# Up projection: all eleven middle gated tiles by seven block products, three of four weight sums on GpSimd, rows with the norm used a tile later

## The chip, the cores and the metric

One NeuronCore of a Trainium2 chip runs the whole kernel. The metric is the device time of one execution in microseconds. The engines are TensorE (PE in the profile; its weight loads are PEld), VectorE (DVE), ScalarE (ACT), GpSimd (POOL) and SyncE (SP), which issues the transfers.

## What is computed

One layer of a streaming encoder for 544 tokens (512 of a prompt, 32 of a decoded chunk), width 1024. Attention comes first; the change lies in the feed-forward part behind it:

```python
x = x + mixed @ w_out
f, conv_state = conv_ffn(rmsnorm(x, n2), w_up, conv_w, conv_b, w_down, conv_prev)

def conv_ffn(h, w_up, conv_w, conv_b, w_down, prev):
    u = h @ w_up                                  # 1024 -> 2 * 2816
    up = jnp.concatenate([prev.astype(u.dtype), u], axis=1)
    c = conv_b + conv_w[0] * up[:, 0:t]
    for j in range(1, CONV_W):                    # CONV_W = 3
        c = c + conv_w[j] * up[:, j:j + t]
    a, g = jnp.split(c, 2, axis=-1)
    return (jax.nn.gelu(a, approximate=False) * g) @ w_down, up[:, -(CONV_W - 1):]
```

The last two rows of `up` of the prompt and of the chunk are outputs too.

## The kernel before

Features lie on the 128 partitions and the 544 tokens along the free axis, in two halves of 272 (`HALVES`). Each float32 operand is split in a high part, rounded for TensorE's fast float32 format, and a low part, the rest; a product is three matmuls, high by high, high by low and low by high (`triple`). The high part is made by a cast on ScalarE or GpSimd, the low part by a subtraction on VectorE (`split`, lines 438 and 439; for weight tiles `prep`, lines 207 to 210).

**The up projection** makes 44 tiles of 128 features: 22 gated tiles, each of a value tile and a gate tile (`gate_order`, the loop of line 1118, index `n`). An ordinary tile (`conv`) takes one weight tile of 512 KB, 2 halves x 8 slices x 3 matmuls of 272 columns, and leaves PSUM by two copies into `us[0]` or `us[1]`. The first `RESCALE2` of them are multiplied by rows without the norm's factor, and VectorE applies it on the way out of PSUM (line 958); from then on the moving rows hold it (`plain`, made by `with_norm`) and ScalarE copies (line 960).

`conv_end` is the convolution for one tile: copies of the last rows into `state_u` on GpSimd, the first tap on ScalarE (line 944), the second on VectorE (line 945), two steps on GpSimd that mend the two columns at the seam between prompt and chunk (lines 947 and 948), the third tap on VectorE (line 950). Then a Gelu on ScalarE for the value tile, or the product with the value on VectorE for the gate tile (line 1128).

**A gated tile by seven block products** (`shared`, for `n` in `SHARED`) takes its value and gate tile together as a 2 x 2 block product over halves of the tokens and pairs of slices: 7 products of 4 slices x 3 matmuls in place of 8. It needs sums of weights (`sums_up`): of the four loaded blocks `wc`, `wd`, `wa`, `wb` (256 KB each) four sums s1 to s4 are made, and the seven operands are each split in high and low part. It needs sums of rows too (`form`), made once from `scaled_x`. ScalarE takes three of the products out of PSUM (lines 1057 to 1061), VectorE forms the four blocks of the result from PSUM and these (lines 1063 to 1070), and `conv_end` follows for both tiles.

**Order.** Engines work through their queues in order; a scheduler sets the order at build time by priorities. `ahead_up(6)` asks for weight operands so that six products' worth are made ahead of the product at hand, at a lower priority than the convolution. Transfers of this kind are issued one behind the other from SyncE. Buffers come from one pool of 50 (`fp`). From `n` = 17 on `take` also splits the gated tiles for the down projection.

Of the kernel before, what the change touches and what calls it, by code (L numbers as in the profile page):

```python
# [11 lines left out]
ALU = mybir.AluOpType  # L12
# [3 lines left out]
NP = 512  # L16
NS = 32
T = NP + NS
# [10 lines left out]
REST = GT - 2 * PAIRS  # L29
UNITS = PAIRS // 2  # L30
H = T // 2
SHARED = (7, 9, 11, 13, 15, 17)
AHEAD_UP = 6
TAKE = {17: 6, 18: 1, 19: 1, 20: 1, 21: 1}
HOMES = lambda g, f: [f] * 3 + [g] * 7 + [f] * 7 + [g] * 6 + [f] * 8 + [g] * 4 + [f] * 3 + [g] * 2
RESCALE2 = 6
EPS = 1e-6
NEG = -1e30
A_BLK = 80
# [109 lines left out]
def body(ctx, tc, a, o):  # L149
# [4 lines left out]
    V, G = nc.vector, nc.gpsimd  # L154
# [16 lines left out]
    def load(out, src, kind="x"):  # L171

        with tc.issue_after(loads[kind].ins) if kind in loads else nullcontext():
            loads[kind] = nc.sync.dma_start(out=out, in_=src)
# [16 lines left out]
    for n, i in enumerate(gate_order):  # L191
        if n not in SHARED:
            sources += [a["w_up"][i], a["w_up"][GT + i]]
# [109 lines left out]
    def col(name, i):  # L303
        return n1[:, i:i + 1] if name == "n1" else cols[:, COL[name][0] + i:COL[name][0] + i + 1]
# [81 lines left out]
    for step in START.split():  # L386
# [3 lines left out]
        else:  # L390
            c = {"": slice(0, T), "a": slice(0, HALVES[0][1]), "b": slice(HALVES[0][1], T)}[step[2:]]
# [45 lines left out]
    def split(dst_hi, dst_lo, src, e=V):  # L437
        nc.scalar.copy(dst_hi, src)  # L438
        e.tensor_tensor(dst_lo, src, rr(dst_hi), ALU.subtract)  # L439
# [485 lines left out]
    state_u = ft.tile([128, UT, 4], F32, name="state_u")  # L925
# [12 lines left out]
    late_g(carry[:, :, 0], carry[:, :, 0], t, ALU.add)  # L938

    def conv_end(m, u, done, own):  # L940
        G.tensor_scalar(state_u[:, m, 0:2], u[:, NP:NP + 2], 1.0, 1.0, ALU.mult, ALU.mult)  # L941
        G.tensor_scalar(state_u[:, m, 2:4], u[:, T:T + 2], 1.0, 1.0, ALU.mult, ALU.mult)
        c = own.tile([128, T], F32, name="s")
        act(c, u[:, 0:T], AF.Identity, scale=col("cw0", m), bias=col("cb", m))
        V.scalar_tensor_tensor(c, u[:, 1:T + 1], col("cw1", m), c, ALU.mult, ALU.add)

        G.tensor_scalar(c[:, NP:NP + 1], carry[:, m, 0:1], 1.0, 1.0, ALU.mult, ALU.mult)
        G.tensor_scalar(c[:, NP + 1:NP + 2], u[:, NP + 2:NP + 3], col("cw1", m), carry[:, m, 1:2],
                        ALU.mult, ALU.add)
        V.scalar_tensor_tensor(c, u[:, 2:T + 2], col("cw2", m), c, ALU.mult, ALU.add)  # L950
        done(c)

    def conv(m, n, done, own):
        u = us[n % 2]

        def evac(s, c0, cn, ps):
            if n < RESCALE2:
                V.tensor_tensor(u[:, 2 + c0:2 + c0 + cn], ps, rstd2[:, c0:c0 + cn], ALU.mult)
            else:
                nc.scalar.copy(u[:, 2 + c0:2 + c0 + cn], ps)  # L960
            if s == 1:
                conv_end(m, u, done, own)
        dense(evac, psa if n % 2 else psd)
# [5 lines left out]
    def with_norm(k):  # L969
        x = fp.tile([128, T], F32, name="s")  # L970
        V.scalar_tensor_tensor(x, x1[k], col("n2", k), rstd2, ALU.mult, ALU.mult)
        h, l = (fp.tile([128, T], F32R, name="s") for _ in range(2))
        split(h, l, x)
        scaled_x.append(x)
        plain.append((h, l))
# [8 lines left out]
    def form(j):  # L984
        t13, t24 = (fp.tile([128, T], F32, name="s") for _ in range(2))
        sums_of(scaled_x[2 * j], scaled_x[2 * j + 1], t13, t24)
        ops = {}
        for e, (names, t) in enumerate(((("t1", "t3"), t13), (("t2", "t4"), t24))):
            h, l = (xp.tile([128, T], F32R, name=f"x{p}{2 * j + e}") for p in "hl")
            split(h, l, t)  # L990
            for i, name in enumerate(names):
                ops[name] = tuple(x[:, i * H:i * H + H] for x in (h, l))
        for e, names in enumerate((("b11", "b12"), ("b21", "b22"))):
            for i, name in enumerate(names):
                ops[name] = tuple(x[:, i * H:i * H + H] for x in plain[2 * j + e])
        forms.append(ops)


    def sums_up():
        for n in range(len(SHARED)):  # L1000
            wc, wd, wa, wb = (fp.tile([128, T], F32, name="s")[:, :512] for _ in range(4))
            for e, w in enumerate((wc, wd, wa, wb)):
                load(w, a["w_shared"][n, :, 512 * e:512 * e + 512])
            s1, s2, s3, s4 = (fp.tile([128, T], F32, name="s")[:, :512] for _ in range(4))

            def both(x):
                h, l = (fp.tile([128, T], F32R, name="s")[:, :512] for _ in range(2))
                split(h, l, x)
                ready_up.append((h, l))
            both(wa)  # L1010
            yield
            V.tensor_tensor(s1, wc, wd, ALU.add)
            V.tensor_tensor(s2, s1, wa, ALU.add)
            both(s2)
            yield
            both(s1)
            yield
            V.tensor_tensor(s3, wc, wa, ALU.add)  # L1018
            both(s3)
            yield  # L1020
            both(wb)
            yield
            V.tensor_tensor(s4, s2, wb, ALU.add)
            both(s4)
            yield
            both(wd)
            yield

    ready_up, used_up = [], []
    making_up = sums_up()  # L1030

    def ahead_up(n):
        while len(ready_up) < len(used_up) + n:
            with tc.high_priority(LATER):
                if next(making_up, 0) == 0:
                    break

    def shared(m1, m2, nth, done1, done2, own):

        pool = psa if nth % 2 else psd  # L1040
        ba, bb, bc = (bank(pool)[:, :H] for _ in range(3))
        p0, q1, e = (ft.tile([128, 272], F32, name=x) for x in ("t_y", "t_b", "t_v"))
        (y11, y12), (y21, y22) = ((u[:, 2:2 + H], u[:, 2 + H:2 + T]) for u in us)
        tt = V.tensor_tensor

        def product(ps, name, first):
            ahead_up(AHEAD_UP)
            h, l = ready_up[len(used_up)]
            used_up.append(name)
            for j in range(KC // 2):  # L1050
                ks = slice(128 * j, 128 * j + 128)
                xh, xl = forms[j][name]
                mm(ps, lhsT=h[:, ks], rhs=xh, start=first and j == 0, stop=False, skip_group_check=True)
                mm(ps, lhsT=h[:, ks], rhs=xl, start=False, stop=False, skip_group_check=True)
                mm(ps, lhsT=l[:, ks], rhs=xh, start=False, stop=j == KC // 2 - 1, skip_group_check=True)
        product(bb, "b11", True)
        nc.scalar.copy(p0, bb)
        product(ba, "t2", True)
        nc.scalar.copy(q1, ba)
        product(bb, "t1", False)  # L1060
        nc.scalar.copy(e, bb)
        product(ba, "t3", False)
        tt(y22, ba, e, ALU.subtract)
        product(bc, "b21", True)
        tt(y11, bc, p0, ALU.add)
        product(bb, "b22", False)
        tt(y12, bb, q1, ALU.subtract)
        conv_end(m1, us[0], done1, own)
        product(ba, "t4", False)
        tt(y21, ba, p0, ALU.subtract)  # L1070
        conv_end(m2, us[1], done2, fp)


# [44 lines left out]
    for n, i in enumerate(gate_order):  # L1118
        part = []
        own = gp if n <= max(SHARED) else fp  # L1120

# [4 lines left out]
        def gate(c, part=part):  # L1126
            v = part[0]
            V.tensor_tensor(v, v, c, ALU.mult)
            gated.append(v)
        if n in SHARED:  # L1130
            shared(i, GT + i, SHARED.index(n), value, gate, own)
        else:
            for e, (m, done) in enumerate(((i, value), (GT + i, gate))):
                conv(m, tile_no, done, own if e == 0 else fp)
                if 1 <= tile_no <= 4:
                    with_norm(2 * tile_no - 2)
                    with_norm(2 * tile_no - 1)
                if tile_no == RESCALE2 - 1:
                    moving[:] = plain
                if RESCALE2 <= tile_no < RESCALE2 + 4:  # L1140
                    form(tile_no - RESCALE2)
                if tile_no >= RESCALE2 + 4 and len(used_up) < 7 * len(SHARED):
                    ahead_up(AHEAD_UP)
# [238 lines left out]
```

## Time and profile before

| what | value |
|---|---|
| median of 3 runs (lowest, highest) | 916.0 us (915.47, 920.13) |
| the profiled execution: time, span | 914.91 us, 913.1 us |
| TensorE busy | 888.1 us (97%) |
| VectorE busy | 743.7 us (81%) |
| ScalarE busy | 582.4 us (64%) |
| GpSimd busy | 421.0 us (46%) |
| granted TensorE clock, mean | 0.998 of full |

The span runs from the first to the last instruction. Busy time is the time in which an engine had at least one instruction under way; the start of one instruction may overlap the end of the one before it on the same engine. The up projection runs from about 536 to 797 us, and the stretch in which tiles by block products and ordinary ones alternate from 619.7 to 743 us.

### The profile page before, as it was taken

Reading aid. Unit: us, or ns where it says so; the run is one execution under the profiler, and the core shown is the slowest. Engines: PE = TensorE matmul, PEld = TensorE weight load, DVE = VectorE, ACT = ScalarE, POOL = GpSimd, SP = SyncE. Lnnn points to the kernel's source line nnn. Section 1 sums busy time; section 2 is a strip of 40 time slices with the busy share of each in tenths; the row PEclk is TensorE's granted clock in tenths of the full one; section 3 lists DMA queues with packets and bytes.
Section 4 is the critical chain, followed back from the end, with each engine's and each line's share of the span. In section 5 each row is a group of like instructions: output and inputs, shape, how many; then the busy total and the mean of one; then the engine's idle time right before and its main releaser. Section 6 shows DMA issues by size and latency. Waiting matters only on the chain.

```text
span 913.1 us, 18964 instructions
## 1 busy us (share of the span) xinstructions
PE 888.1 (97%) x7013; PEld 872.7 (96%) x7013; DVE 743.7 (81%) x1512; ACT 582.4 (64%) x1399; POOL 421.0 (46%) x577
## 2 busy tenths in 40 slices
PE   8979999999999999999999999999999999999998
PEld 7979899989989999999999999999999999999998
DVE  7798877768888897998865559998778778899996
ACT  5668787678878677777774236565555566645552
POOL 4625557465876777766551206444434344200100
PEclk9999999999999999999999999999999999999999
DMA  7222132322334443444415222253323012222342
GB/s 225 91 81 96 54 97 81 104 79 75 115 115 120 140 124 103 123 127 136 124 59 180 93 72 91 70 183 100 99 83 117 24 59 95 83 94 93 118 147 66
DMA packets 41742, 94.38 MB, mean 103 GB/s; under 512 B 5137, under 2 KB 16433, under 8 KB 41649
## 3 DMA queue, kind: packets, MB, share of 16 engines
q1 hardware_dynamic: 41648, 93.17, 32.5%
q8 instruction: 55, 0.90, 0.4%
q14 instruction: 39, 0.31, 0.1%
HBM read 80.48 MB, written 7.10 MB: 96 GB/s over the span
## 4 chain that ended last, share of the span: by engine, by line
PE 76%; DVE 9%; ACT 4%; POOL 4%; issue 2%; DVEq 0%; POOLq 0%; ACTq 0%
PE ps L90 73%; PE ps L94 3%; DVE q L454 1%; DVE zn L430 1%; ACT p L493 1%; DVE p L509 1%; POOL p L501 1%; DVE w_lo L210 1%; POOL t_sql L422 1%; POOL z L429 1%; DVE t_b L325 1%; DVE k L439 1%; POOL s L707 0%; POOL t_sqh L421 0%; DVE pt_l L520 0%
## 5 line engine op out<-in xcount | busy, mean ns | idle before, releaser
L90 PE MATMUL ps<-xh,w_lo 128*128 128x272 f32 x1024 | 297.5, 292 | 5.9 <-DVE w_lo L210 5.9
L90 PE MATMUL ps<-xh,w_hi 128*128 128x272 f32 x1024 | 297.5, 293 | 1.9 <-ACT z L420 1.7
L90 PE MATMUL ps<-xl,w_hi 128*128 128x272 f32 x1024 | 297.8, 292 | 0.3 <-DVE xl L333 0.3
L90 PE MATMUL ps<-s,w_hi 128*128 128x272 f32 x1088 | 205.3, 288 | 1.2 <-ACT w_hi L209 1.2
L90 PEld LDWEIGHTS ps<-xh,w_lo 128*128 128x128 f32 x1024 | 194.2, 190 | 7.2 <-DVE w_lo L210 6.7
L90 PEld LDWEIGHTS ps<-xh,w_hi 128*128 128x128 f32 x1024 | 193.9, 190 | 4.3 <-ACT z L420 2.0
L90 PEld LDWEIGHTS ps<-xl,w_hi 128*128 128x128 f32 x1024 | 194.5, 190 | 1.3 <-DVE xl L333 0.7
L90 PEld LDWEIGHTS ps<-s,w_hi 128*128 128x128 f32 x1088 | 169.9, 188 | 1.6 <-ACT w_hi L209 1.6
L90 PE MATMUL ps<-s,w_lo 128*128 128x272 f32 x544 | 154.1, 287 | 0.0
L210 DVE TENSOR_TENSOR w_lo<-w_raw,w_hi 128x1024 fp32r<-128x1024 f32 (+2 forms) x100 | 128.3, 1283 | 27.0 <-POOL w_hi L207 13.9
L90 PE MATMUL ps<-s 128*128 128x272 f32 (+1 forms) x843 | 115.2, 291 | 1.7 <-DVE s L379 1.7
L90 PEld LDWEIGHTS ps<-s 128*128 128x128 f32 x843 | 109.9, 189 | 2.2 <-DVE s L379 1.7
L207 POOL TENSOR_SCALAR w_hi<-w_raw 128x1024 fp32r<-128x1024 f32 (+2 forms) x62 | 67.0, 1081 | 92.6 <-PE ps L90 68.9
L90 PEld LDWEIGHTS ps<-s,w_lo 128*128 128x128 f32 x544 | 101.8, 188 | 0.1
L501 POOL TENSOR_SCALAR p<-p,rc 128x256 f32<-128x256 f32 (+3 forms) x128 | 74.9, 602 | 41.3 <-DVE rc L499 36.6
L941 POOL TENSOR_SCALAR state_u<-u 128x2 f32<-128x2 f32 x44 | 30.3, 689 | 118.0 <-ACT u L960 41.1
L493 ACT ACTIVATE p<-p,nm 128x256 f32<-128x256 f32 (+3 forms) x128 | 65.6, 516 | 27.9 <-DVE nm L490 27.8
L438 ACT CAST s<-s 128x512 fp32r<-128x512 f32 (+1 forms) x80 | 49.7, 633 | 39.1 <-DVE s L1018 10.6
L209 ACT CAST w_hi<-w_raw 128x1024 fp32r<-128x1024 f32 x38 | 40.0, 1053 | 44.6 <-PE ps L90 29.7
L439 DVE TENSOR_TENSOR s<-s 128x512 fp32r<-128x512 f32 (+1 forms) x80 | 55.7, 710 | 2.2 <-ACT s L438 2.1
L90 PE MATMUL ps<-k,q 128*128 128x256 f32 (+2 forms) x256 | 52.2, 308 | 2.6 <-DVE s L528 0.8
L422 POOL TENSOR_TENSOR t_sql<-t_sq,t_sqh 128x272 fp32r<-128x272 f32 x52 | 52.6, 1012 | 3.7
(175 smaller groups left out, 1801.1 us busy)
## 6 DMA issues: line engine op xcount, KB each, us to landing
w_raw<-in_w_in SPq DMA_DIRECT2D x50, 512.0 KB, 3.4
w_raw<-in_w_up SPq DMA_DIRECT2D x32, 512.0 KB, 3.4
w_raw<-in_w_pair SPq DMA_DIRECT2D x16, 512.0 KB, 3.4
s<-in_w_shared SPq DMA_DIRECT2D x24, 256.0 KB, 4.2
k<-k SPq DMA_DIRECT2D x40, 128.0 KB, 2.3
bias<-in_rel SPq DMA_DIRECT2D x16, 256.0 KB, 3.0
w_raw<-in_w_out SPq DMA_DIRECT2D x8, 512.0 KB, 3.5
s<-in_x SPq DMA_DIRECT2D x15, 272.0 KB, 5.8
```

The lines of the kernel that those rows point to most:

```text
L90: return self.nc.tensor.matmul(out, lhsT=lhsT, rhs=rhs, **kw)
L94: return self.nc.tensor.transpose(out, src, ident)
L207: G.tensor_scalar(hi[:, c], raw[:, c], 1.0, 1.0, ALU.mult, ALU.mult)
L209: nc.scalar.copy(hi[:, c], raw[:, c])
L210: V.tensor_tensor(lo[:, c], raw[:, c], rr(hi)[:, c], ALU.subtract)
L325: V.scalar_tensor_tensor(b, st, eps, b, ALU.add, ALU.mult)
L422: G.tensor_tensor(sql, sq, rr(sqh), ALU.subtract)
L438: nc.scalar.copy(dst_hi, src)
L439: e.tensor_tensor(dst_lo, src, rr(dst_hi), ALU.subtract)
L493: act(p[:, sl], p[:, sl], AF.Exp, bias=nm[:, t:t + 1], accum_out=sm[:, t:t + 1])
L501: G.tensor_scalar(p[:, sl], p[:, sl], rc[:, t:t + 1], 1.0, ALU.mult, ALU.mult)
L941: G.tensor_scalar(state_u[:, m, 0:2], u[:, NP:NP + 2], 1.0, 1.0, ALU.mult, ALU.mult)
```

## The change

`SHARED` names all of the gated tiles 7 to 17 in place of 7, 9, 11, 13, 15 and 17, so tiles 8, 10, 12, 14 and 16 are made by block products too, and no ordinary tile stands between them. The layout of the shared weights on the host follows `SHARED`. Of the four weight sums of a tile s1, s3 and s4 move from VectorE to GpSimd; s2 stays. `RESCALE2` goes from 6 to 7: a seventh ordinary tile is multiplied by rows without the norm's factor, and `form` and the first `ahead_up` come a tile later. The two copies into `state_u` become one instruction of two pieces of two columns.

```diff
-SHARED = (7, 9, 11, 13, 15, 17)
+SHARED = tuple(range(7, 18))
...
-RESCALE2 = 6
+RESCALE2 = 7
...
     def conv_end(m, u, done, own):
-        G.tensor_scalar(state_u[:, m, 0:2], u[:, NP:NP + 2], 1.0, 1.0, ALU.mult, ALU.mult)
-        G.tensor_scalar(state_u[:, m, 2:4], u[:, T:T + 2], 1.0, 1.0, ALU.mult, ALU.mult)
+        G.tensor_scalar(state_u[:, m].rearrange("p (e r) -> p e r", e=2),
+                        u[:, NP - 30:].rearrange("p (e c) -> p e c", e=2)[:, :, 30:], 1.0, 1.0, ALU.mult, ALU.mult)
...
-            V.tensor_tensor(s1, wc, wd, ALU.add)
+            G.tensor_tensor(s1, wc, wd, ALU.add)
             V.tensor_tensor(s2, s1, wa, ALU.add)
...
-            V.tensor_tensor(s3, wc, wa, ALU.add)
+            G.tensor_tensor(s3, wc, wa, ALU.add)
...
-            V.tensor_tensor(s4, s2, wb, ALU.add)
+            G.tensor_tensor(s4, s2, wb, ALU.add)
```

## Rows read from the trace of the kernel before

**Rows 1.** Windows: stretch, length, each engine busy us (instructions), PEclk, DMA.

```profile
619.70:743.00 123.30, 123.30 (x987) 123.30 (x986) 97.56 (x148) 67.88 (x123) 51.42 (x86) 1.00 0.26 82
743.00:797.00 54.00, 54.00 (x434) 54.00 (x433) 44.71 (x72) 34.75 (x59) 20.42 (x38) 1.00 0.25 80
```

**Rows 2.** Waits of PE, 535 to 820 us: total, times, longest.

```profile
PE ps L90 <- ACT w_hi L209: 1.2, 2, 0.7
```

**Rows 3.** Timeline of ACT, 579 to 582 us: start, us, instruction.

```profile
579.64 0.39 ACT L960 COPY u<-ps 128x272 f32<-128x272 f32 x1 [0.26 <-PE ps L90]
579.92 1.05 ACT L209 CAST w_hi<-w_raw 128x1024 fp32r<-128x1024 f32 x1
580.87 0.39 ACT L960 COPY u<-ps 128x272 f32<-128x272 f32 x1
581.15 1.06 ACT L209 CAST w_hi<-w_raw 128x1024 fp32r<-128x1024 f32 x1
```

**Rows 4.** Timeline of DVE, 655.5 to 661.2 us.

```profile
655.11 0.44 DVE L1070 TENSOR_TENSOR u<-ps,t_y 128x272 f32<-128x272 f32 x1 [1.08 <-PE ps L90]
655.47 0.78 DVE L945 SCALAR_TENSOR_TENSOR s<-u,cols,s 128x544 f32<-128x544 f32 x1
656.16 0.69 DVE L439 TENSOR_TENSOR s<-s 128x512 fp32r<-128x512 f32 x1
656.76 0.69 DVE L1023 TENSOR_TENSOR s<-s 128x512 f32<-128x512 f32 x1
657.36 0.79 DVE L945 SCALAR_TENSOR_TENSOR s<-u,cols,s 128x544 f32<-128x544 f32 x1
658.24 0.79 DVE L950 SCALAR_TENSOR_TENSOR s<-u,cols,s 128x544 f32<-128x544 f32 x1
658.94 1.22 DVE L210 TENSOR_TENSOR w_lo<-w_raw,w_hi 128x1024 fp32r<-128x1024 f32 x1
660.08 0.69 DVE L439 TENSOR_TENSOR s<-s 128x512 fp32r<-128x512 f32 x1
660.93 0.79 DVE L950 SCALAR_TENSOR_TENSOR s<-u,cols,s 128x544 f32<-128x544 f32 x1 [0.17 <-POOL s L948]
```

**Rows 5.** Instructions by line, DVE, 617 to 743 us: busy, mean ns.

```profile
L1128 DVE TENSOR_TENSOR s<-s 128x544 f32<-128x544 f32 x12 | 8.6, 720 | 0.3
```

**Rows 6.** Timeline of DVE, 99.5 to 104 us.

```profile
100.30 3.52 DVE L430 SCALAR_TENSOR_TENSOR zn<-t_b,z 128x272 f32<-128x272 f32 x1 [0.25 <-POOL z L429]
```

**Rows 7.** Timeline of POOL, 99.5 to 104 us.

```profile
100.25 0.40 POOL L501 TENSOR_SCALAR p_s<-p_s,rc 128x160 f32<-128x160 f32 x1
100.62 1.05 POOL L207 TENSOR_SCALAR w_hi<-w_raw 128x1024 fp32r<-128x1024 f32 x1
...
102.75 0.77 POOL L422 TENSOR_TENSOR t_sql<-t_sq,t_sqh 128x272 fp32r<-128x272 f32 x1
```

**Rows 8.** Single lines, whole span: duration ns min/median/max.

```profile
L707 POOL TENSOR_TENSOR s<-s x8: 1349/1359/1571, 112.7 to 259.6; 128x544 f32<-128x544 f32 x8
...
L429 POOL TENSOR_TENSOR z<-z,t_y x52: 754/776/1311, 37.6 to 447.0; 128x272 f32<-128x272 f32 x52
...
L430 DVE SCALAR_TENSOR_TENSOR zn<-t_b,z x52: 406/474/3518, 38.4 to 450.2; 128x272 f32<-128x272 f32 x52
...
L325 DVE SCALAR_TENSOR_TENSOR t_b<-ps,eps,t_b x56: 477/496/503, 27.6 to 546.5; 128x272 f32<-128x272 f32 x56
...
L948 POOL TENSOR_SCALAR s<-u,cols,carry x44: 335/786/2521, 550.8 to 793.7; 128x1 f32<-128x1 f32 x44
```

**Rows 9.** Timeline of POOL, 655.5 to 661.2 us.

```profile
656.33 0.57 POOL L947 TENSOR_SCALAR s<-carry 128x1 f32<-128x1 f32 x1 [2.10 <-DVE s L945]
656.88 1.32 POOL L948 TENSOR_SCALAR s<-u,cols,carry 128x1 f32<-128x1 f32 x1
658.31 0.77 POOL L947 TENSOR_SCALAR s<-carry 128x1 f32<-128x1 f32 x1
659.06 1.84 POOL L948 TENSOR_SCALAR s<-u,cols,carry 128x1 f32<-128x1 f32 x1
```

**Rows 10.** Waits of DVE, 617 to 743 us.

```profile
DVE s L950 <- POOL s L948: 6.6, 18, 0.6
DVE u L1070 <- PE ps L90: 3.7, 4, 1.1
```

**Rows 11.** Page, DMA issues: size, median us to landing.

```profile
s<-in_w_shared SPq DMA_DIRECT2D x24, 256.0 KB, 4.2
```

## The prediction

> **What bounds the kernel now.** I read the table of the page first: TensorE is busy through nearly all of the span, so a gain has to be a gain of TensorE's time in the stretch that changes. That stretch runs from the first of the six tiles by block products to the last, 619.7 to 743 us. The windows view shows TensorE without a gap there, at full clock, and VectorE busy 97.6 us of the 123.3 [rows 1]: TensorE sets the pace, and VectorE has 26 us to spare. TensorE's only waits near by are two short ones at 580 us, 1.2 us together, for a high half of a weight tile that ScalarE casts late [rows 2].
>
> The pace: 987 matmuls in 123.3 us are 0.1249 us each. A tile by block products has 7 x 4 x 3 = 84 of them, 10.49 us; a pair of ordinary tiles 2 x 2 x 8 x 3 = 96, 11.99 us. The stretch by the code's counts is 6 x 10.49 + 5 x 11.99 = 122.9 us.
>
> **Part one, the five further tiles, on TensorE.** Eleven tiles of 84 matmuls take 115.4 us: 7.5 us less than 122.9. That is all that the change can gain there, and only while TensorE stays the bound.
>
> **Part two, the norm a tile later.** At 580 us ScalarE's queue holds a copy of a projected half behind which the cast of the next weights stands; the copy waits for TensorE, and TensorE then waits for the cast [rows 3]. With the limit at 7, both halves of that tile leave through VectorE instead, and the cast is free to go earlier. I credit the whole 1.2 us; if the same queue forms one tile later it is 0. On VectorE it adds two multiplies from PSUM at about 0.36 us each, and moves the forming of operands and the first sums by one tile of 6.0 us. Three ordinary tiles, 18 us, still lie between the first sums and the first product, so the six operands that are made ahead can still be ready: no cost. The merged state copies take 44 instructions off GpSimd; nobody waits for them, so nothing.
>
> **Part three, VectorE and GpSimd.** This decides. VectorE's instructions overlap a little, so I cost them from start to start in a run of neighbours [rows 4]: a subtraction or sum of 128x512 0.60 us, the two convolution steps 0.69 and 0.70, a difference taken from PSUM 0.36, a low half of a weight tile 1.14; the gate's product 0.72 long [rows 5], about 0.63 by the same overlap.
>
> A tile by block products asks VectorE for 11 x 0.60 + 2 x 0.69 + 2 x 0.70 + 0.63 + 4 x 0.36 = 11.45 us; a pair of ordinary tiles for 2 x 1.14 + 2.78 + 0.63 = 5.69. Six and five of these make 97.2 us, which is the 97.6 of the window [rows 1]. The five ordinary pairs are what gives VectorE its rest now. Eleven block tiles at 11.45 would be 126 us against TensorE's 115.4. With three sums gone to GpSimd it is 9.65 us a tile, 106 in all: by busy time alone it fits.
>
> It fits only if a sum on GpSimd costs VectorE nothing, and the trace says otherwise. At 100.3 us a VectorE product of two SBUF inputs took 3.52 us, with GpSimd busy all that time with five instructions; it ended 0.30 us after the last of them [rows 6, 7]. Its median is 0.47 us [rows 8]. So it did not run slower, it stood still until GpSimd was through. The other way round: a GpSimd step on one column takes 0.34 us at its fastest [rows 8], but 1.32 and 1.84 us when VectorE ran instructions with two SBUF inputs one after another [rows 4, 9], and it ended with VectorE's first pause. An instruction of the same shape that reads one input from PSUM never took over 0.50 us in 56 cases [rows 8]. The two engines exclude each other on work from two SBUF inputs; work from PSUM is free.
>
> The price of one sum on GpSimd: 128x544 takes 1.36 us and 128x272 0.78 us [rows 8]; on the line between, 128x512 is 1.29, and it can't well be under 0.78 or over 1.57, the longest of eight. The blocked instruction of rows 6 finished 0.17 us earlier than its own length after the block (0.30 instead of 0.47), so I take 1.11 us of VectorE's time lost for a sum. On VectorE it cost 0.60.
>
> The period of a tile, then. Floor: VectorE's work from two SBUF inputs, 8 x 0.60 + 2.78 + 0.63 = 8.21 us, and three holds of 1.11, with everything from PSUM hidden under them: 11.54. Ceiling: all of VectorE's 9.65, three whole sums of 1.29, and two waits for GpSimd's column steps at 6.6 / 18 = 0.37 each [rows 10]: 14.26. I take 9.65 + 3.33, less half of the PSUM work (0.72) that falls under a hold, plus the two waits (0.74): 13.0 us. That is over TensorE's 10.49, so VectorE and GpSimd together become the bound, and the waits of VectorE for TensorE [rows 10] turn round.
>
> What is ahead counts once: six of seven operands of the first tile are ready when it starts, 6/7 of (8 x 0.60 + 3.33) = 7.0 us. The stretch becomes 11 x 13.0 - 7.0 = 136.0 us, where it was 122.9: +13.1. Behind it VectorE is some 5 us late, and the 54 us that follow have 9.3 us of rest for it [rows 1]: between 0 and 3, I take 1.5. Who waits: behind a VectorE instruction that waits for a sum stand the low halves of the next operands, and for those TensorE waits. Behind GpSimd's sums stand the column steps for the two seam columns, for which VectorE's last convolution step waits.
>
> The loads stay off the path: four of 256 KB for a tile as now, 4.2 us to landing [rows 11], a tile's period ahead; in bytes a block tile loads as much as an ordinary pair. ScalarE, at 67.9 of 123.3 us [rows 1], has room.
>
> **The sum.** The profiled execution took 914.9 us (span 913.1 and 1.8 around it), and the median of the runs is 1.1 above it. 914.9 + 13.1 - 1.2 + 1.5 = 928.3; on the median's footing 929 us. With the floor, 11 x 11.54 - 7.0 = 119.9, 3.0 less than now: 916.0 - 3.0 - 1.2 = 912. With the ceiling, 149.9: 916.0 + 27.0 + 3 = 946.
>
> **A rule beside it.** Rows 6 and 7 show a block over five GpSimd instructions, rows 9 one over two of VectorE's: an engine that goes on without a pause keeps the other out. The Trainium skill (SBUF — State Buffer, "Who interferes with whom") has an exclusive lock too, but lets the first to issue hold it for its one instruction. By that, GpSimd would not starve and each sum would cost VectorE its whole length: 9.65 + 3 x 1.29 = 13.5 a tile, some 935 us.
> A second rule speaks for the change: the same skill (Perfetto Trace Analysis, "Optimizing Scalar/DVE Operations") says that off-loading a saturated VectorE, even to GpSimd, may help, and adds that their shared port may undo it. Rows 6 and 7 bear out the caveat.
>
> **The rivals.**
> A, TensorE stays the bound (the other sign). It holds if the 37 us that 33 sums hold (33 x 1.11) go into time in which VectorE works from PSUM (11 x 1.44 = 16 us) or waits anyway, so that the period falls to 10.5 us. For it: VectorE had 26 us of rest in this stretch. Against it: of the rest of 115.4 - 106 = 9 and the 16 us of PSUM work only 25 us can take them in, under 37. Then 916.0 - 7.5 - 1.2 = 907 us. 20%.
> B, the floor: GpSimd's holds take in all the PSUM work and no column step is waited for. For it: the order is planned well ahead. Against it: the column steps are waited for now, 18 times [rows 10]. 912 to 918, no change. 17%.
> C, the ceiling or worse: sums in GpSimd's one queue put loads (4.2), the first sum, the second and the fourth in series, and the period is 14.3 or more. For it: GpSimd's queue would hold both the column steps and the sums. Against it: six operands are made ahead. 946 us. 8%.
> The forecast, 920 to 942: 55%.
>
> **How the numbers follow.** The likeliest case gives 929. From 908, in the middle of A's spread, to 946 about 17 in 100 are left out, half of A and part of C; the likeliest alone runs from 920 to 942. Half a per cent, 4.6 us, is about what can be told from no change. Faster by more: A, 20%. Within it: B, 17%. Slower by more: forecast and C, 63%.
>
> **What would show it.** Right: in the stretch of eleven tiles TensorE's busy share falls to about 0.85, it waits for the low halves (the subtraction of line 439), VectorE's 128x512 and 128x544 instructions show lengths well over 0.69 and 0.79, the three sums on GpSimd 1.3 us and more, and the stretch is near 136 us. The waits for the weight cast at 580 us are gone. Wrong: TensorE without gaps over 115 us, or VectorE's instructions at their old lengths beside GpSimd's sums, which would mean that sums of this shape don't exclude VectorE as in rows 6.

## The result and the profile after

The changed kernel takes 967.5 us in the median of 4 runs (963.6 to 969.0), beside 916.1 us for the kernel before on the same chip: ratio 1.0545, 95% interval 1.0501 to 1.0588. That is slower by 5.45%, some 50 us (51.4 between the medians, 48.6 between the profiled spans), where 929 us had been forecast; it is above the range. The profiled execution took 963.58 us, its span 961.7.

The windows view of the changed kernel answers to [rows 1, 2]: first the stretch with the two waits for the weight cast, then the stretch of the eleven tiles as far as TensorE has gaps (the last products of the eleventh come later, among those of ordinary tiles).

```profile
550.00:600.00 50.00, 50.00 (x402) 50.00 (x401) 45.71 (x72) 30.67 (x46) 22.27 (x28) 1.00 0.31 97
...
619.00:786.00 167.00, 124.27 (x869) 116.84 (x870) 125.24 (x169) 70.76 (x131) 71.32 (x92) 0.96 0.20 64
```

The first row has no gap any more: the credit for the norm a tile later holds. The second is the loss: 869 matmuls at the old pace of 0.1249 us would be 108.5 us, and the stretch is 167, so 58.5 us are lost. Less the 7.5 and the 1.2 that the change does save, that is 49.8 us, beside 48.6 between the spans: all of the difference lies here. But no engine is busy through the stretch: VectorE has 125 of 167 us, GpSimd 71. So it is not a matter of load alone, and the waits say what each engine stands for (changed kernel, 620 to 785 us; total, times, longest):

```profile
POOL s L947 <- DVE s L945: 65.0, 20, 7.3
ACT s L944 <- DVE u L1067: 39.0, 10, 4.5
...
PE ps L90 <- DVE s L439: 30.2, 17, 2.4
...
ACT t_b L1059 <- PE ps L90: 26.7, 9, 3.8
DVE s L439 <- ACT s L438: 23.2, 11, 3.1
ACT s L438 <- DVE s L1013: 20.6, 9, 2.4
DVE s L945 <- ACT s L944: 12.2, 18, 0.9
```

Everybody waits for everybody: GpSimd and ScalarE for VectorE, TensorE for VectorE's low halves, ScalarE for TensorE, VectorE for ScalarE. Waits of this kind can be those of a chain in a ring: each tile's end releases the next tile's beginning. VectorE's timeline at the end of one tile shows where it would close:

```profile
710.32 0.44 DVE L1063 TENSOR_TENSOR u<-ps,t_v 128x272 f32<-128x272 f32 x1
710.67 0.43 DVE L1067 TENSOR_TENSOR u<-ps,t_b 128x272 f32<-128x272 f32 x1
712.02 1.21 DVE L945 SCALAR_TENSOR_TENSOR s<-u,cols,s 128x544 f32<-128x544 f32 x1 [0.91 <-ACT s L944]
713.14 0.43 DVE L1070 TENSOR_TENSOR u<-ps,t_y 128x272 f32<-128x272 f32 x1
713.49 0.70 DVE L439 TENSOR_TENSOR s<-s 128x512 fp32r<-128x512 f32 x1
714.12 0.68 DVE L1013 TENSOR_TENSOR s<-s 128x512 f32<-128x512 f32 x1
```

Line 1070 takes the last difference of this tile out of PSUM. The very next instruction, line 439 at 713.49, makes the low half of the next tile's first operand. TensorE's timeline shows what each tile waits for: at 701.97 this tile starts again behind its second low half, at 714.25 the next one behind its first:

```profile
701.97 0.52 PE L90 MATMUL ps<-xh,s 128*128 128x272 f32 x2 [2.33 <-DVE s L439]
...
714.25 1.53 PE L90 MATMUL ps<-s 128*128 128x272 f32 x10 [1.19 <-DVE s L439]
```

So nothing is made ahead at the border of two tiles: products, then differences, then the next tile's operands, then its products. (At the first border and the last, one low half does come ahead of line 1070.) In the kernel before, four low halves of the next tile by block products come ahead of line 1070, which is at 655.11 there [rows 4], and an ordinary pair still lies between:

```profile
646.86 0.68 DVE L439 TENSOR_TENSOR s<-s 128x512 fp32r<-128x512 f32 x1
...
650.40 1.28 DVE L439 TENSOR_TENSOR s<-s 128x512 fp32r<-128x512 f32 x2
...
653.35 0.68 DVE L439 TENSOR_TENSOR s<-s 128x512 fp32r<-128x512 f32 x1
```

VectorE's queue is not the only one. ScalarE's timeline in the changed kernel has the cast of the same operand, at 711.89, behind a first tap that waits 3.91 us for line 1067:

```profile
711.14 0.84 ACT L944 ACTIVATE s<-u,cols 128x544 f32<-128x544 f32 x1 [3.91 <-DVE u L1067]
711.89 0.60 ACT L438 CAST s<-s 128x512 fp32r<-128x512 f32 x1
```

GpSimd's timeline over the same end of a tile has the next tile's first sum behind two copies of this tile's last rows, just before it at 710.84 and 711.19, which wait for lines 1063 and 1067 in the same way:

```profile
711.35 1.29 POOL L1012 TENSOR_TENSOR s<-s 128x512 f32<-128x512 f32 x1
713.31 0.19 POOL L947 TENSOR_SCALAR s<-carry 128x1 f32<-128x1 f32 x1 [0.67 <-DVE s L945]
713.48 1.37 POOL L948 TENSOR_SCALAR s<-u,cols,carry 128x1 f32<-128x1 f32 x1
```

The exclusion is there too. VectorE's line 945 at 712.02 takes 1.21 us beside the sum that ends at 712.64, where it takes 0.78 in [rows 4]. The step on one column, 0.34 us at its fastest [rows 8], takes 1.37 us while VectorE runs lines 439 and 1013.

For the comparisons below I use one row of each kernel, the window 650 to 730 us, and read the period of a tile (the time from one tile to the next) from it: 80 us x 84 / number of matmuls. The changed kernel's row gives 16.6 us:

```profile
650.00:730.00 80.00, 57.86 (x404) 54.56 (x405) 58.07 (x81) 33.01 (x62) 30.41 (x42) 0.96 0.18 57
```

### The profile page after: what moved, and what is told of

The parts are those of the page before. It is cut to its first block, busy times and chain, and to the rows that moved or that the text cites. A ratio compares the mean times of both kernels' runs of the same rounds, so it can differ in the third digit from the quotient of the medians.

```text
span 961.7 us, 18994 instructions
## 1 busy us (share of the span) xinstructions
PE 894.3 (93%) x6953; PEld 872.2 (91%) x6953; DVE 779.7 (81%) x1546; ACT 588.8 (61%) x1417; POOL 439.0 (46%) x566
## 4 chain that ended last, share of the span: by engine, by line
PE 62%; DVE 16%; ACT 6%; issue 5%; POOL 5%; DMA 0%; POOLq 0%; ACTq 0%; DVEq 0%
PE ps L90 59%; PE ps L94 3%; DVE s L439 3%; DVE s L945 2%; ACT s L944 1%; ACT p L493 1%; POOL s L947 1%; DVE w_lo L210 1%; DVE q L454 1%; DVE p L509 1%; DVE zn L430 1%; DVE s L950 1%; POOL s L948 1%; POOL p L501 1%; DVE t_b L325 1%
## 5 line engine op out<-in xcount | busy, mean ns | idle before, releaser
L90 PE MATMUL ps<-s 128*128 128x272 f32 (+1 forms) x1023 | 143.7, 292 | 12.4 <-DVE s L439 9.5
L90 PE MATMUL ps<-s,w_hi 128*128 128x272 f32 x736 | 138.3, 288 | 0.0
L90 PEld LDWEIGHTS ps<-s,w_hi 128*128 128x128 f32 x736 | 114.9, 188 | 0.0
L90 PE MATMUL ps<-xh,s 128*128 128x272 f32 x372 | 82.7, 308 | 32.6 <-DVE s L439 20.7
L439 DVE TENSOR_TENSOR s<-s 128x512 fp32r<-128x512 f32 (+1 forms) x115 | 89.3, 796 | 23.3 <-ACT s L438 23.2
L90 PE MATMUL ps<-s,w_lo 128*128 128x272 f32 x368 | 103.9, 287 | 0.0
L90 PEld LDWEIGHTS ps<-xh,s 128*128 128x128 f32 x372 | 64.3, 203 | 37.0 <-DVE s L439 22.6
L947 POOL TENSOR_SCALAR s<-carry 128x1 f32<-128x1 f32 x44 | 28.0, 636 | 111.3 <-DVE s L945 108.7
L90 PEld LDWEIGHTS ps<-s,w_lo 128*128 128x128 f32 x368 | 68.8, 189 | 0.0
L944 ACT ACTIVATE s<-u,cols 128x544 f32<-128x544 f32 x44 | 37.0, 842 | 43.0 <-DVE u L1067 40.8
```

The costliest lines, as they stand in the source:

```text
L90: return self.nc.tensor.matmul(out, lhsT=lhsT, rhs=rhs, **kw)
```

## The experiments

Three causes were in question: the order of the queues, as above; loads or buffers that come late; the sums on GpSimd, by their length or by exclusion. Ratios are to the kernel before, beside which each ran (913.6 to 914.3 us).

**e1, the sums back on VectorE.** The changed kernel with

```diff
-            G.tensor_tensor(s1, wc, wd, ALU.add)
+            V.tensor_tensor(s1, wc, wd, ALU.add)
```

and the same for s3 and s4.

> The change, but the three weight sums back on VectorE. Theory 1 (buffers): the pool of 50 buffers is full in the eleven tiles, so the operands of a tile are made only after the tile before it has been consumed, and the chain through one tile is walked end to end; sums on VectorE shorten that chain by some 2 to 3 us of 16.6, so about 935 to 945 us. Theory 2 (the exclusion of VectorE and GpSimd alone, as the prediction had it): without GpSimd's holds the period is VectorE's own 11.45 us and 0.7 of waits, 918 to 922 us.

948.9 us, 1.0382 (1.0344 to 1.0420). That is outside both expectations, a little above the first. The sums on GpSimd account for 1.6% of the 5.45; 3.8% stay without them. The window row of e1, a period of 15.6 us:

```profile
650.00:730.00 80.00, 61.94 (x430) 57.31 (x429) 61.26 (x103) 36.16 (x68) 13.33 (x30) 0.96 0.20 67
```

VectorE is busy 61 of 80 us and still the period is far over its 11.45 us of work.

**e2, the sums on GpSimd alone.** The kernel before, six tiles, with `V` turned into `G` in the three lines.

> The kernel before with one part of the change: its six block tiles, the three sums on GpSimd. Theory 1: with ordinary tiles between, the operands still run ahead and VectorE has 26 us of rest for 18 holds of 1.11 us less 18 x 0.60, 9 us: 914 to 918 us, no change. Theory 2: the same. Theory 3 (a sum on GpSimd is late by itself, and TensorE waits for it each time): 18 waits of a microsecond or more, 930 us or more.

914.5 us, 1.0009 (0.9994 to 1.0023): no difference. With an ordinary pair between tiles TensorE loses nothing to it, as e2's window shows, so the sums on GpSimd are not late by themselves:

```profile
619.00:743.00 124.00, 123.90 (x990) 123.69 (x989) 99.22 (x134) 68.57 (x124) 63.40 (x104) 1.00 0.25 84
```

**e3 and e4, eight more buffers for the operands.** The residual rows give up their buffers until the down projection:

```diff
+    x1 = [fp.tile([128, T], F32, name="s") for _ in range(KC)]
+    for m in range(KC):
+        load(x1[m], a["x"][m])
```

e3 is this in the changed kernel, e4 in e1.

> The change with eight more buffers free in the eleven tiles: the residual rows are not held through the up projection, and the down projection adds freshly loaded rows of x instead (this leaves out the attention's part of the residual). Theory 1: operands are made ahead again, what remains is the exclusion of VectorE and GpSimd at about 13 us a tile: 925 to 935 us. Theory 2: buffers don't matter, within 1% of 967 us.

> Both: eight more buffers free as in the run before (the attention's part of the residual left out) and the three sums back on VectorE. Theory 1: the period is VectorE's 11.45 us and some waits, 12 us: 915 to 920 us, and the gap to the run before is the price of the sums on GpSimd. Theory 2: the same time as with the sums on VectorE and the buffers as they were.

979.2 us (1.0714) and 965.4 us (1.0563), both over the kernels that they start from and outside what was expected of them. The loads are issued some 20 us before their first use in e3, and the window 650 to 730 of e3 holds the same 404 matmuls as the changed kernel's. Buffers and loads are not what the tiles wait for: that theory falls. The extra time lies behind the stretch (in both TensorE waits 12.8 us once, for the residual sum of the down projection).

**e5 and e6, VectorE's order by hand.** Each difference from PSUM is issued behind the low half that is five products ahead. e5 has the sums on VectorE, e6 on GpSimd as in the change.

```diff
-                split(h, l, x)
+                nc.scalar.copy(h, x)
+                lows.append(V.tensor_tensor(l, x, rr(h), ALU.subtract))
...
-        tt = V.tensor_tensor
+        def tt(*x):
+            with tc.issue_after(lows[min(len(used_up) - 1 + 5, len(lows) - 1)].ins):
+                V.tensor_tensor(*x)
```

> The three sums on VectorE, and VectorE's queue ordered by hand: each of the four differences from PSUM is issued behind the low half of the operand five products ahead, so the next tile's operands no longer stand behind this tile's last difference. Theory 3 (order: the queue makes each tile a closed loop, products, differences, then the next tile's operands): the period falls from 15.3 us to VectorE's own 11.45 and some waits, 916 to 925 us. Theory 1 (buffers), already weak: no change, 945 to 950 us.

> The change as it is, sums on GpSimd, with the same order by hand. Theory 3: the period falls from 16.6 us to the 13.0 of the prediction, in which VectorE and GpSimd exclude each other: 927 to 935 us. If order is not what holds it: within 1% of 967 us.

e5: 936.6 us, 1.0252 (1.0223 to 1.0282). e6: 944.0 us, 1.0333 (1.0303 to 1.0363). Both miss what was expected of the order, 916 to 925 and 927 to 935 us: it is a part of the loss and not the whole. With the work unchanged it is worth 5.45 - 3.33 = 2.1% (19 us) with the sums on GpSimd and 1.3% (12 us) with them on VectorE. The edit names VectorE's instructions alone, but ScalarE's casts move ahead of its first taps with them, so the runs price the order of the queues together. The window rows, first e5 (period 13.8 us):

```profile
650.00:730.00 80.00, 68.58 (x486) 61.98 (x485) 69.26 (x117) 40.29 (x74) 23.19 (x34) 1.00 0.24 80
```

and e6 (14.5 us):

```profile
650.00:730.00 80.00, 64.27 (x465) 60.39 (x464) 69.84 (x93) 38.12 (x72) 44.90 (x51) 0.98 0.21 70
```

VectorE is now busy 69 to 70 of 80 us, up from 61 and 58. The periods are nearer to its work, but still over TensorE's 10.49. The sums on GpSimd cost 0.8% (7 us) more than on VectorE.

**e7 and e8, a larger lead asked for.** `AHEAD_UP = 13` in place of 6, in e1 (e7) and in the changed kernel (e8).

> The three sums on VectorE, and 13 operands asked for ahead in place of 6, no order by hand. The queue of VectorE then has the next tile's first low halves ahead of the last difference. Theory 3: part of the gain of the order by hand, 920 to 940 us. If buffers hold it: no change or slower, 949 us or more.

> The change with 13 operands asked for ahead in place of 6. Theory 3: 935 to 955 us. If buffers hold it: no change or slower, 967 us or more.

950.3 us, 1.0402, and 956.4 us, 1.0469. e7 misses its expectation, 920 to 940 us: a lead of nearly two tiles, asked for in the program, is no better than e1. It helps e8 by 0.8%. So asking for a larger lead does not do what the order by hand does. Why is not shown: in e7's trace line 1070 comes ahead of lines 1065 and 1067, so the scheduler moved the tile's products as well.

**e9, the norm a tile later alone.** The kernel before with `RESCALE2 = 7` and the merged state copies, six tiles.

> The kernel before with only the norm used a tile later and the state copies merged; six tiles by block products as before. The prediction credited 1.2 us for this: theory 1 says the two waits of TensorE at 580 us go and nothing comes in their place, so 912.4 us beside 913.6, ratio 0.9987. Theory 2 says that the waits go, but the time is given back behind them (VectorE starts on the block operands a tile later), ratio 1.000 or more.

912.15 us, 0.9981 (0.9972 to 0.9989): 1.8 us faster (1.0 to 2.6), where 1.2 had been credited; the run does not tell the norm from the merged copies. This is the one part of the change that pays, and the version that beats both kernels. Its window, to be held against the TensorE bound, has no gap (period 10.5 us by the matmuls):

```profile
650.00:730.00 80.00, 80.00 (x641) 80.00 (x641) 64.90 (x99) 45.37 (x80) 26.99 (x44) 1.00 0.24 81
```

**e10 and e11, without the three sums.** e10 is e5, e11 the changed kernel, each with the lines of s1, s3 and s4 taken out:

```diff
-            V.tensor_tensor(s2, s1, wa, ALU.add)
+            V.tensor_tensor(s2, wc, wa, ALU.add)
...
-            both(s1)
+            both(wc)
...
-            both(s3)
+            both(wc)
...
-            both(s4)
+            both(s2)
```

> As e5 (VectorE's order by hand), with the first, third and fourth weight sum of a tile left out: their operands are cast from tiles that are there already, so the products are as many but not the reference's. Theory 1 (with the order mended, VectorE's own work sets the period): three sums of 0.60 us less, so a period of 13.76 - 1.80 = 11.96 us, and 936.6 - 11 x 1.8 = 917 us (914 to 921). Theory 2 (the period of 13.76 us is set by the chain of load, cast and low half): sums off the chain give little, period over 13.0 us, 928 us or more. Theory 3 (TensorE becomes the bound as soon as the sums are gone): period 10.5 us, 905 us or less.

> The changed kernel, its queue order left as it is, with the same three sums left out (not on GpSimd, not on VectorE). Theory 1 (queue order closes a loop through each tile, whoever makes the sums): TensorE still waits at the head of every tile, and the run is at least 8 us above e10, 925 to 940 us, a period of 12.7 to 14.0 us. Theory 2 (the loop is nothing but the sums' time on it): with the sums gone the order no longer matters, and the run is within 3 us of e10.

e10: 913.9 us, 1.0004 (0.9993 to 1.0014). e11: 923.0 us, 1.0104 (1.0090 to 1.0119). e10 is 2.5% (22.7 us) under e5, 0.69 us for each of 33 sums, which VectorE starts 0.60 us apart: with the order mended, VectorE's work goes into the period at about its own price, and the second theory, in which the chain sets the period whatever the sums do, falls. How much of the 0.69 is work and how much a shorter way to s2's operand is not told apart, since the second sum no longer waits for the first. e11 stays 9 us above e10, so the order costs even where nobody makes sums; its 923 us are a little under the 925 expected. The window rows, first e10 (11.5 us):

```profile
650.00:730.00 80.00, 76.52 (x585) 73.68 (x584) 69.21 (x117) 48.17 (x89) 26.11 (x42) 1.00 0.31 104
```

and e11 (12.8 us):

```profile
650.00:730.00 80.00, 72.32 (x523) 66.98 (x524) 64.59 (x107) 43.18 (x83) 20.17 (x37) 1.00 0.27 91
```

**e12, seven tiles.** e9 with the order of e5 and

```diff
-SHARED = (7, 9, 11, 13, 15, 17)
+SHARED = (7, 9, 11, 13, 14, 16, 17)
```

> The kernel before with the norm a tile later, the merged copies, VectorE's order by hand, and seven tiles by block products in place of six (positions 7, 9, 11, 13, 14, 16, 17), all sums on VectorE. Each further tile by block products saves TensorE 1.5 us. Theory 1: a tile by block products that follows another directly costs up to 13.76 - 10.49 = 3.3 us, less what the lead from an ordinary tile takes in; with two such places 912.4 - 1.5 + 0 to 6.6: 911 to 917.5 us, and under 912.4 only if the lead takes in both. Theory 2 (the order by hand alone removes the cost of neighbours): 911 us or less, faster than e9.

914.55 us, 1.0012 (1.0003 to 1.0021), 2.8 us over e9 by the ratios. The two places where tiles follow each other cost 2.8 + 1.5 = 4.3 us, some 2.2 each, if the order by hand is free for the other tiles (no run has it with six): a direct neighbour costs more than a tile by block products saves.

**e13 and e14, what a sum on GpSimd costs by itself.** e10 with the three sums made on GpSimd and read by nobody (e13), or with two copies of one input in place of each (e14):

```diff
+            G.tensor_scalar(s1, wc, 1.0, 1.0, ALU.mult, ALU.mult)
+            G.tensor_scalar(s1, wd, 1.0, 1.0, ALU.mult, ALU.mult)
```

> As e10 (VectorE's order by hand, no product waits for the first, third or fourth sum), but GpSimd still makes the three sums of each tile and nothing reads them. Against e10's 913.9 us. Theory 1 (a sum on GpSimd keeps VectorE out, whoever waits for it): 33 sums at 0.5 to 1.11 us of VectorE each, 930 to 950 us, and VectorE's low halves longer than the 0.69 us that they take undisturbed. Theory 2 (the price is the sum's 1.3 us in the chain of a tile): with nobody waiting it is gone, 914 to 918 us.

> As e13, with each unused sum on GpSimd replaced by two unused copies of the same size, which read one input each: GpSimd is about as busy (a copy of 128x1024 took 1.05 us, so two of 128x512 about 1.1). Theory 1 in its narrow form (only work from two SBUF inputs excludes): 914 to 918 us and low halves of 0.69 us. Theory 3 (any GpSimd work beside VectorE stretches it): within 5 us of e13.

e13: 939.5 us, 1.0278 (1.0261 to 1.0294). e14: 928.9 us, 1.0161 (1.0144 to 1.0178). In e13 nobody waits for the sums, and they still cost 2.7% (25 us), 0.76 us each; that they are read as well adds only the 0.55% (5 us) from e13 to e6. They could also cost by standing in GpSimd's queue ahead of the column steps that VectorE waits for. The instructions by line, 619 to 760 us, rule that out for the third tap, first e10, then e13 (busy, mean ns, then the waits):

```profile
L950 DVE SCALAR_TENSOR_TENSOR s<-u,cols,s 128x544 f32<-128x544 f32 x23 | 18.0, 784 | 4.4 <-POOL s L948 4.4
L950 DVE SCALAR_TENSOR_TENSOR s<-u,cols,s 128x544 f32<-128x544 f32 x19 | 24.9, 1310 | 4.3 <-POOL s L948 4.2
```

The waits are the same, the instructions are longer: 1.31 us instead of 0.78, and by the same view the second tap 0.96 instead of 0.78, the low half 0.84 instead of 0.69, the gate's product 0.81 instead of 0.72. Times the counts in e13 that is 25 us in this window, as much as the run lost. The exclusion is shown, and VectorE's timeline in e13 shows its form (the order by hand too, in the last two rows, with a low half ahead of a difference):

```profile
695.20 0.78 DVE L950 SCALAR_TENSOR_TENSOR s<-u,cols,s 128x544 f32<-128x544 f32 x1
696.23 1.79 DVE L950 SCALAR_TENSOR_TENSOR s<-u,cols,s 128x544 f32<-128x544 f32 x1 [0.25 <-POOL s L948]
697.94 1.78 DVE L1009 TENSOR_TENSOR s<-s 128x512 fp32r<-128x512 f32 x1
...
703.26 0.68 DVE L1009 TENSOR_TENSOR s<-s 128x512 fp32r<-128x512 f32 x1
703.86 0.43 DVE L1047 TENSOR_TENSOR u<-ps,t_y 128x272 f32<-128x272 f32 x1
```

GpSimd's in the same stretch:

```profile
690.87 1.29 POOL L1024 TENSOR_TENSOR s<-s 128x512 f32<-128x512 f32 x1
...
696.16 1.27 POOL L1013 TENSOR_TENSOR s<-s 128x512 f32<-128x512 f32 x1
697.40 1.77 POOL L1019 TENSOR_TENSOR s<-s 128x512 f32<-128x512 f32 x1
```

Read the two side by side. The sum at 696.16 runs at its full speed and holds line 950, which takes 1.79 us instead of 0.78; then line 950 holds the second sum, and that holds the low half of line 1009, 1.78 us instead of 0.68. They take turns, an instruction each. The sum at 690.87 falls into VectorE's wait for TensorE and costs nothing: in this tile two of three are paid.

e14 lies between the theories: its copies of one input are not free. Two of them on GpSimd's timeline in e14:

```profile
702.33 0.61 POOL L1013 TENSOR_SCALAR s<-s 128x512 f32<-128x512 f32 x1
703.03 0.97 POOL L1014 TENSOR_SCALAR s<-s 128x512 f32<-128x512 f32 x1
```

and VectorE's timeline beside them:

```profile
702.41 1.11 DVE L950 SCALAR_TENSOR_TENSOR s<-u,cols,s 128x544 f32<-128x544 f32 x1 [0.25 <-POOL s L948]
703.44 1.09 DVE L1009 TENSOR_TENSOR s<-s 128x512 fp32r<-128x512 f32 x1
```

It is the same taking of turns. Line 950 ends 0.58 us after the first copy, as it ended 0.59 after the first sum in e13 (698.02 against 697.43); line 1009 ends 0.53 after the second, where it was 0.55. Only the holds are shorter, because a copy takes 0.61 us and a sum 1.27. The copies cost 1.6% (14 us), 0.43 for a pair, so the narrow form, that both sides need two SBUF inputs, falls: for GpSimd one is enough.

## Why the prediction was wrong

The sign and most mechanisms held, the size did not: 13 us were forecast, 50 came. The 5.45% come apart by the runs: order of the queues 2.1% (changed kernel to e6), the sums as operands that are waited for 0.55% (e6 to e13), exclusion 2.7% (e13 to e10), and 0.0% from e10 to the kernel before (eleven tiles without the three sums take as long as six with them). The shares go by this order of taking the causes away; with the sums first they are 4.4% (changed kernel to e11) and 1.0% for the order (e11 to e10).

**The step that failed** is "What is ahead counts once: six of seven operands of the first tile are ready when it starts", and with it the answer to rival C, "six operands are made ahead". It took the period for a sum of loads, with the lead as a buffer against everything else. The lead of `ahead_up(6)` is one of the program's order only. With no ordinary tile in between, VectorE's queue holds the next tile's first operand behind this tile's last difference, and the lead is zero at all borders but the first and the last. So the period is the length of a ring, 16.6 us, and not 13.0. Three differences with the work unchanged show what the order costs (changed kernel to e6 19 us, e1 to e5 12, e11 to e10 9). Rows 4 show the differences and the low halves in one queue, but I didn't ask which low half would stand behind line 1070 once the pair between was gone. Of the 37 us that the forecast missed the order is 19; the other 18 or so lie in the period that is left with the order mended.

Not even the first tile has the lead of that sentence. By VectorE's and TensorE's timelines of the changed kernel one low half had ended when the first product began, where the kernel before had six:

```profile
610.37 0.68 DVE L439 TENSOR_TENSOR s<-s 128x512 fp32r<-128x512 f32 x1
...
614.99 0.69 DVE L439 TENSOR_TENSOR s<-s 128x512 fp32r<-128x512 f32 x1
```

```profile
615.24 1.68 PE L90 MATMUL ps<-s 128*128 128x272 f32 x12
```

The credit of 7.0 us came out near its size all the same: from the first copy of the first tile, at 619.93, to that of the second, at 630.51, it is 10.6 us, where later tiles take 16.4 and more. It came by another way than the one forecast.

**The terms of the period.** With the order mended the period was 14.5 us in e6's window, and 14.1 from copy to copy in the tiles at full clock: above the 13.0, near the ceiling of 14.26. The price of a sum was taken too high, 1.11 us against 0.76, since, in the tile shown, one in three falls into a pause. The base was taken too low: 9.65 less 0.72 and plus 0.74, but e10 with just that work on VectorE has a period of 11.5. The 1.8 us between are VectorE's waits for casts and first taps, for TensorE and for the column steps (8.4 and 3.4, 4.9, 4.4 us of e10's stretch from 619 to 760); I had priced the last alone.

**The rule beside it.** I wrote that an engine which goes on without a pause keeps the other out, from rows 6, 7 and 9. In e13 and e14 the engines take turns after each instruction instead. That is how the Trainium skill has it (SBUF — State Buffer, "Who interferes with whom"): the first to issue holds the port for its whole instruction, and a GpSimd instruction that reads SBUF is enough to collide with VectorE's two inputs. The trace of e13 agrees for sums (1.78 us where 0.68 is undisturbed), that of e14 for copies (1.09). The 13.5 us a tile worked out by that rule was nearer to e6 than my 13.0, but by luck: it takes 1.29 us a sum where 0.76 was paid, which stands in for the waits that the base lacks. The rule is not all: rows 6, and the column step of 1.37 us shown above, were held over several instructions of the other engine, and no run here settles why.

**What held.** TensorE is not the bound, so rival A (907 us) falls; B falls too. The pace and the 7.5 us are borne out by the balance of the window, the 1.2 us by e9 (1.8 measured). TensorE waits for low halves, as said. Its busy share of the stretch is 0.74 by the row, not 0.85. The loads stayed off the path (e3). C came nearest: a series in the queues, but closed through VectorE, not GpSimd (e1 has it without the sums).

## What to carry to other kernels

A lead that the program asks for exists only if the in-order queue of each engine holds the next tile's first operands ahead of this tile's last results; before interleaved work is taken out, ask what will then stand directly behind the last instruction of a tile. If so, cost the period as the longer of the engine's load and the ring. Sums from two SBUF inputs that went from VectorE to GpSimd still cost here about as much as on VectorE, 0.76 us against 0.69, so count such work as moved only where VectorE would pause.

## What the runs showed of the hardware that was not expected

From 665 us on the periods of the changed kernel alternate. The windows view, one row from the first copy of a tile to that of the next:

```profile
665.05:681.52 16.47, 11.56 (x86) 10.83 (x84) 12.62 (x18) 7.07 (x13) 6.97 (x10) 1.00 0.21 61
681.52:699.43 17.91, 12.95 (x86) 12.18 (x84) 12.62 (x18) 7.06 (x14) 6.96 (x10) 0.90 0.21 61
699.43:715.87 16.44, 11.60 (x86) 10.80 (x84) 12.60 (x18) 7.06 (x14) 6.96 (x10) 1.00 0.20 66
715.87:733.67 17.80, 12.87 (x86) 12.12 (x84) 12.61 (x18) 7.07 (x14) 6.96 (x10) 0.90 0.16 54
```

The work is the same; the granted clock is not. In the slow ones it falls to half:

```profile
683.00:685.00 2.00, 0.93 (x4) 0.93 (x5) 1.62 (x2) 0.03 (x1) 0.46 (x1) 0.73 0.28 71
685.00:686.00 1.00, 1.00 (x6) 1.00 (x6) 0.00 (x0) 0.00 (x0) 0.00 (x0) 0.50 0.00 0
```

The instruction behind its wait in this tile, by TensorE's timeline:

```profile
684.07 0.82 PE L90 MATMUL ps<-xh,s 128*128 128x272 f32 x2 [2.34 <-DVE s L439]
```

At the end of its wait of 2.34 us in this tile TensorE runs at 1.2 instead of 2.4 GHz for some 3 us, and the period is 1.4 us longer. The wait of 2.33 us in the next tile, shown further up at 701.97, costs no clock. In the kernel before the clock stays at 1.00 in the stretch [rows 1]. Four periods of the changed kernel have a clock of 0.90 or 0.91, so its gaps cost it some 5.5 us a second time. That is part of what the order costs, but not all of it goes with the order: e6's row still shows 0.98. Why some of these waits cost the clock and others of the same length do not, no run here settles.
